# Where the eight turned pieces of a token block lie in PSUM, and how many last expert terms are summed at the end

## The chip, the cores and the metric

The kernel runs on one core of one Trainium2 chip. The metric is the device time of one execution in microseconds (us); the median of several executions is compared. Engines are named as in the profile: PE (TensorE, matmuls), PEld (its weight loads), DVE (VectorE), ACT (ScalarE), POOL (GpSimd) and SP (SyncE, which issues the DMAs). PSUM, the memory that PE writes, has eight banks of 512 f32 columns in each of 128 partitions.

## The reference, cut to what matters

256 tokens of width 1024 go through a first block (attention and mLSTM, then PEER, a sum over 128 x 128 experts) and through two layers of a second block (a mixer and a convolutional GLU, here "ffn"). Between any two of these stages stands the same join: the stage's output is added to the running tokens x, and x is normalised for the next stage.

```
def rmsnorm(x, g):
    y = xf * lax.rsqrt(jnp.mean(xf * xf, axis=-1, keepdims=True) + EPS)
    return (y * g.astype(jnp.float32)).astype(x.dtype)
...
        act = jax.nn.gelu(jnp.einsum('thkd,td->thk', expert_u[eidx], xb).astype(jnp.float32), approximate=False)
        return jnp.einsum('thk,thkd->td', (g * act).astype(xb.dtype), expert_v[eidx])
...
        x = x + gt2 * peer(h2, w_pq[l], sub_keys[l], expert_u[l], expert_v[l])
```

## The kernel before

Matmuls run in split precision: a number is held as a high and a low half, and `mm3` (L274 to L276) issues high x high, high x low and low x high as three matmuls; `mm` (L279) is a single one. The split of a weight is made by ACT (`wh`, L289) and DVE or POOL (`wl`, L293). `bank()` hands out one of the eight PSUM banks.

The join (L714 on) works on two blocks b of 128 tokens each. For each block `update` adds the stage's output to x (L741 to L749, DVE); `norm` squares x on ACT (`jj`, L724), makes 1/rms by a chain of ten small DVE operations (L731, then L402 to L410) and puts it on a diagonal matrix `jdg` on ACT (L759); `features` then multiplies each of eight 128 x 128 pieces of x by `jdg`, which turns the piece (features onto partitions) and scales it. Each piece goes to a bank of its own, ACT reads it there into the high half (L768: `hh`, in the join ahead of PEER `r`), and DVE reads it again for the low half (L778: `hl`; ahead of PEER, where a bias is added, the pair L782 and L783). There are five such joins with features: ahead of PEER (tiles `x`, in the profile at 264 to 283 us), ahead of the mixer of layer 0 and 1 (at 1107 and 1497 us), and ahead of the ffn of layer 0 and 1 (at 1300 and 1687 us); a sixth writes the output and turns nothing.

In the joins of the mixers and the ffns a first sum that needs the features (the mixer's values, with weights `sh`, `sl`; the ffn's first products, with `sth`, `stl`) is issued block by block within the join, as `early`: for the mixer 32 matmuls with `hh` and then 16 with `hl` in each block, for the ffn 16 and 8. The join ahead of PEER has none, and 15 plain matmuls of the identity (`warm`) stand there instead.

PEER ends with a sum over 128 terms into four banks (two token blocks by two halves of the columns). Its last `TAILV` terms are not summed as they come: their weights are split into four tiles each (`wtail`: two halves of `wth` and two of `wtl`, from a pool of 40 such tiles that 16 tiles of the next mixer's values share), and `finish` then sums bank after bank, so that the first token block is complete while the second is still summed. The activations of a term (`k`) lie in tiles of which there are six.

The order of the instructions on each engine is set by a list scheduler ahead of time; the `issue_after` lines at the end of `join` pin a few of them. A tile's buffer, a bank too, is taken again when its last user is done, and engines that use one bank are kept apart by semaphores.

Of the kernel before, what the change touches and what calls it, by code (L numbers as in the profile page):

```python
# [19 lines left out]
P = 128  # L20
# [24 lines left out]
WARM2 = 12  # L45
DLAG = 4
TAILF = 5
TAILV = 5
NRAW = 6
NWIDE = 40  # L50
AVF = 4, 6, 8, 10
# [208 lines left out]
class Kern:  # L260
# [453 lines left out]
    def join(self, ys, row, post, out=None, scale=None, bias=None, pair=None, early=None):  # L714
# [47 lines left out]
        def features(b):  # L762

            xs, o, low = self.X[2 * b:2 * b + 2], slice(b * P, (b + 1) * P), []
            for c in range(KD):
                pt = self.bank()[:, :P]
                self.mm(pt, xs[c // 4][:, c % 4 * P:(c % 4 + 1) * P], dgs[b])
                self.mark = nc.scalar.activation(hT[c].hi[:, o], pt, AF.Copy if bias is None else AF.Identity,  # L768
                                                 bias=0.0 if bias is None else bias[:, c:c + 1],
                                                 scale=scale[:, c:c + 1])  # L770
                low.append(pt)
            yield
            for c, pt in enumerate(low):
                if c == LOS:
                    yield
                hi, lo = hT[c].hi[:, o], hT[c].lo[:, o]
                if bias is None:
                    nc.vector.scalar_tensor_tensor(lo, pt, scale[:, c:c + 1], hi.bitcast(F32),  # L778
                                                   op0=OP.mult, op1=OP.subtract)
                else:  # L780
                    h32 = self.S([P, P], name="h32")
                    nc.vector.tensor_scalar(h32, pt, scale[:, c:c + 1], bias[:, c:c + 1], op0=OP.mult, op1=OP.add)  # L782
                    nc.vector.tensor_tensor(lo, h32, hi.bitcast(F32), op=OP.subtract)  # L783
            yield

        after = self.tc.issue_after
        dgs = []
        u0, u1, n0, n1, f0, f1 = update(0), update(1), norm(0), norm(1), features(0), features(1)
        next(u0)
        next(u0)  # L790
# [36 lines left out]
    def peer(self, ys, gb):  # L827
# [166 lines left out]
        for n, j in enumerate(order):  # L994
# [8 lines left out]
            hh = parted[n]  # L1003
            if n >= NKEY - TAILV:
                parts.append((hh, self.wtail(src)))
# [1029 lines left out]
```

## Time and profile before

| what | us |
|---|---|
| median of 3 executions (lowest, highest) | 1892.14 (1888.83, 1896.81) |
| the profiled execution | 1893.5 |
| its span in the trace | 1891.7 |
| PE busy in it | 1823.5 |
| DVE, ACT busy | 1305.4, 1004.2 |
| PE idle for `jdg` (L759), five times, in all | 15.0 |
| PE idle for `hl` (L778), four times, in all | 5.5 |

PE is the engine that is nearly always busy. What it idles is small, and a part of that idling lies in the five joins. In a timeline row the first number is the start, the second the length, then engine, line and operation, and at the end in brackets how long the engine had been idle and what released it.

### The profile page before, as it was taken

What the parts mean: (1) busy time and instruction counts of PE and PEld (TensorE: products, weight loads), DVE (VectorE), ACT (ScalarE), POOL (GpSimd) and SP (SyncE); (2) the same over time, 40 slices, a digit from 0 to 9 for tenths busy, and PEclk for the clock granted to TensorE, in tenths of its full rate; (3) what the DMA queues carried; (4) which work ended last, traced back from release to release, by engine and by line L of the source; (5) the groups of instructions that cost most, each with busy time, mean ns of one, the idle gap of its engine ahead of it and who ended that gap; (6) DMA issues with size and microseconds to landing.
All of it is one profiled execution on the core that took longest, in us unless ns stands there. A gap on an engine that the chain in (4) does not pass through costs nothing.

```text
span 1891.7 us, 32791 instructions
## 1 busy us (share of the span) xinstructions
PE 1823.5 (96%) x12634; PEld 1621.5 (86%) x12634; DVE 1305.4 (69%) x3029; ACT 1004.2 (53%) x1856; POOL 176.6 (9%) x119
## 2 busy tenths in 40 slices
PE   7999989999999999999999999998999999989998
PEld 6776579999999999888888788987999899879997
DVE  4535677997888896555555656767787666767775
ACT  4525544435666665444444646456666464456663
POOL 0000002321000000000000003400100033201000
PEclk9999989999999999999999999999999999999999
DMA  8722454454445446555555744313676233125571
GB/s 308 255 102 101 152 173 135 162 173 138 162 159 165 161 164 203 189 188 187 186 188 183 231 137 135 112 56 112 202 233 217 74 130 128 56 82 184 195 232 57
DMA packets 85101, 302.93 MB, mean 160 GB/s; under 512 B 10096, under 2 KB 10992, under 8 KB 84816
## 3 DMA queue, kind: packets, MB, share of 16 engines
q1 hardware_dynamic: 84944, 300.83, 48.1%
q8 instruction: 99, 1.62, 0.3%
q14 instruction: 58, 0.48, 0.1%
HBM read 298.56 MB, written 2.10 MB: 159 GB/s over the span
## 4 chain that ended last, share of the span: by engine, by line
PE 82%; DVE 12%; ACT 3%; DMA 1%; issue 1%; SPq 0%; POOLq 0%; POOL 0%; DVEq 0%; ACTq 0%
PE b L274 22%; PE b L276 21%; PE b L275 21%; PE b L279 14%; DVE wl L293 3%; PE b L1160 1%; DMA raw<-in_wv 1%; ACT wh L289 1%; PE b L524 1%; PE b L1351 1%; DMA raw<-in_w_ada 1%; DVE eq L1091 0%; DVE tm L1024 0%; DVE u L1980 0%; DVE jt L741 0%
## 5 line engine op out<-in xcount | busy, mean ns | idle before, releaser
L289 ACT ACTIVATE wh<-raw 128x1024 fp32r<-128x1024 f32 x457 | 483.7, 1060 | 532.0 <-PE b L275 214.4
L293 DVE TENSOR_TENSOR wl<-raw,wh 128x1024 fp32r<-128x1024 f32 x414 | 524.2, 1267 | 274.0 <-ACT wh L289 273.5
L276 PE MATMUL b<-r,wl 128*128 128x256 f32 (+1 forms) x1216 | 345.0, 284 | 9.1 <-DVE wl L293 9.1
L274 PE MATMUL b<-r,wh 128*128 128x256 f32 (+1 forms) x1216 | 351.9, 289 | 0.0
L275 PE MATMUL b<-r,wh 128*128 128x256 f32 x1152 | 323.7, 281 | 0.0
L274 PE MATMUL b<-hh,wh 128*128 128x256 f32 x1056 | 301.6, 286 | 1.8 <-DVE ast L1676 1.8
L276 PE MATMUL b<-hh,wl 128*128 128x256 f32 x1056 | 299.6, 284 | 1.8 <-DVE wl L293 1.7
L275 PE MATMUL b<-hl,wh 128*128 128x256 f32 x1056 | 298.6, 283 | 0.0
L276 PEld LDWEIGHTS b<-r,wl 128*128 128x128 f32 x1216 | 231.0, 190 | 11.8 <-DVE wl L293 10.3
L274 PEld LDWEIGHTS b<-r,wh 128*128 128x128 f32 x1216 | 231.1, 190 | 3.1 <-issue 1.5
L293 POOL TENSOR_TENSOR wl<-raw,wh 128x1024 fp32r<-128x1024 f32 x43 | 105.7, 2459 | 1219.5 <-ACT wh L289 947.8
L275 PEld LDWEIGHTS b<-r,wh 128*128 128x128 f32 x1152 | 218.6, 190 | 0.0
L274 PEld LDWEIGHTS b<-hh,wh 128*128 128x128 f32 x1056 | 202.2, 191 | 4.5 <-DVE ast L1676 2.2
L276 PEld LDWEIGHTS b<-hh,wl 128*128 128x128 f32 x1056 | 202.2, 191 | 3.1 <-DVE wl L293 3.0
L275 PEld LDWEIGHTS b<-hl,wh 128*128 128x128 f32 x1056 | 202.3, 192 | 1.4
L275 PE MATMUL b<-wl,k 128*128 128x512 f32 x492 | 194.9, 396 | 1.5 <-DVE wl L293 1.4
L274 PE MATMUL b<-wh,k 128*128 128x512 f32 x492 | 194.7, 396 | 0.0
L276 PE MATMUL b<-wh,k 128*128 128x512 f32 x492 | 194.6, 395 | 0.0
L275 PEld LDWEIGHTS b<-wl,k 128*128 128x128 f32 x492 | 92.4, 188 | 24.7 <-DVE wl L293 2.6
L274 PEld LDWEIGHTS b<-wh,k 128*128 128x128 f32 x492 | 92.4, 188 | 22.5 <-ACT wh L289 0.3
L276 PEld LDWEIGHTS b<-wh,k 128*128 128x128 f32 x492 | 92.4, 188 | 22.3
L1980 DVE SCALAR_TENSOR_TENSOR u<-b,vec,u 128x255 f32<-128x255 f32 (+1 forms) x176 | 84.3, 479 | 9.1 <-ACT u L1978 6.5
(492 smaller groups left out, 3019.0 us busy)
## 6 DMA issues: line engine op xcount, KB each, us to landing
raw<-in_eu SPq DMA_DIRECT2D x128, 512.0 KB, 3.8
raw<-in_ev SPq DMA_DIRECT2D x128, 512.0 KB, 3.6
raw<-in_fi SPq DMA_DIRECT2D x88, 512.0 KB, 4.6
raw<-in_w_ada SPq DMA_DIRECT2D x48, 512.0 KB, 5.3
raw<-in_wi SPq DMA_DIRECT2D x48, 512.0 KB, 3.9
raw<-in_fo SPq DMA_DIRECT2D x44, 512.0 KB, 4.7
raw<-in_w SPq DMA_DIRECT2D x16, 512.0 KB, 6.1
raw<-in_w_pq SPq DMA_DIRECT2D x16, 512.0 KB, 4.2
```

The lines of the kernel that those rows point to most:

```text
L274: mm(out, L.hi, R.hi, start=start, stop=False, skip_group_check=True)
L275: mm(out, L.hi, R.lo, start=False, stop=False, skip_group_check=True)
L276: self.lastmm = mm(out, L.lo, R.hi, start=False, stop=stop, skip_group_check=True)
L279: self.nc.tensor.matmul(out, l, r, start=start, stop=stop, skip_group_check=True)
L289: nc.scalar.activation(dst.hi, src, AF.Copy)
L293: e.tensor_tensor(dst.lo, src, dst.hi.bitcast(F32), op=OP.subtract)
L524: nc.tensor.matmul(pa[32 * j:32 * j + 32, :P], self.s2[:, 4 * h + k], wa[:, k, m * P:(m + 1) * P], start=(k == 0), stop=(k == 3), tile_pos ...
L1160: nc.tensor.matmul(pa[32 * j:32 * j + 32], self.s2[:, k], wa[:, j % 2 * 512:(j % 2 + 1) * 512], start=(k == 0), stop=(k == KD - 1), tile_p ...
L1351: nc.tensor.transpose(pt[:, sc * P:(sc + 1) * P], Pm[:, sc * P:(sc + 1) * P], self.ident)
L1980: nc.vector.scalar_tensor_tensor(u[:, g, j:], src[:, :T - j], self.v2("fc", (2 - j) * 44 + i), u[:, g, j:], op0=OP.mult, op1=OP.add)
```

## The change

The eight pieces of a token block no longer take eight banks: four of them lie side by side in one bank (`quad`), so that a block takes two. `TAILV` goes from 5 to 7: two more of PEER's terms are held back for `finish`. Line numbers behind the edit grow by two (L768 becomes L770, L778 L780, L782 and L783 L784 and L785).

```diff
-TAILV = 5
+TAILV = 7
...
             for c in range(KD):
-                pt = self.bank()[:, :P]
+                if c % 4 == 0:
+                    quad = self.bank()
+                pt = quad[:, c % 4 * P:(c % 4 + 1) * P]
                 self.mm(pt, xs[c // 4][:, c % 4 * P:(c % 4 + 1) * P], dgs[b])
```

The first place is PE's queue at the first token block of the join ahead of layer 0's mixer (`jdg` turns pieces; `sh` and `sl` by `hh` are the values; the number behind `b_` tells the bank's tile). Before:

```order
L279 MATMUL b_12161<-jdg_12157,r_9330 128x128 [waits Activation_49]
L279 MATMUL b_12164<-jdg_12157,r_9330 128x128
L279 MATMUL b_12167<-jdg_12157,r_9330 128x128 [waits PE_49]
L279 MATMUL b_12170<-jdg_12157,r_9330 128x128 [waits PE_49]
L279 MATMUL b_12173<-jdg_12157,r_9331 128x128 [waits DVE_49]
L279 MATMUL b_12176<-jdg_12157,r_9331 128x128
L279 MATMUL b_12179<-jdg_12157,r_9331 128x128 [waits DVE_49]
L279 MATMUL b_12182<-jdg_12157,r_9331 128x128 [waits DVE_49]
L279 MATMUL b_12214<-sh_11743,hh_12110 128x260 [waits DVE_49]
```

and now:

```order
L279 MATMUL b_12157<-jdg_12153,r_9318 128x128 [waits Activation_49]
L279 MATMUL b_12166<-jdg_12153,r_9319 128x128 [waits DVE_49]
L279 MATMUL b_12157<-jdg_12153,r_9318 128x128 [waits Activation_49]
L279 MATMUL b_12204<-sh_11731,hh_12106 128x260 [waits PE_49]
L279 MATMUL b_12204<-sl_11732,hh_12106 128x260
L279 MATMUL b_12205<-sh_11731,hh_12106 128x260 [waits PE_49]
L279 MATMUL b_12205<-sl_11732,hh_12106 128x260
L279 MATMUL b_12157<-jdg_12153,r_9318 128x128 [waits Activation_49]
L279 MATMUL b_12204<-sh_11735,hh_12108 128x260
L279 MATMUL b_12204<-sl_11736,hh_12108 128x260
```

The eight turning matmuls stood in a row, and each into its own bank; now the second piece of bank b_12157 waits for ACT, as do the third and all that follow in a bank, and matmuls of the values stand between them. Only the first piece of each of the two banks goes ahead without such a wait. The ffn's joins read likewise, with two matmuls (`sth`, `stl`) between pieces.

The second place is ACT's queue in the join ahead of PEER (L768, now L770, reads pieces; `wh` splits a weight; `jj` and `jdg` belong to the second token block). Before, from the sixth piece of the first block on:

```order
L724 ACTIVATE jj_2518,jss_2517<-x_77 128x512
L724 ACTIVATE jj_2520,jss_2517<-x_77 128x512 [waits DVE_49]
L289 ACTIVATE wh_2711<-raw_2709 128x1024 [waits DMAHW3_49]
L289 ACTIVATE wh_2744<-raw_2742 128x1024 [waits DMAHW4_49]
L289 ACTIVATE wh_2791<-raw_2789 128x1024 [waits DMAHW5_49]
L759 ACTIVATE jdg_2562<-ident_59,rq_2525 128x128 [waits DVE_49]
```

and now, from the third piece of the first block on:

```order
L770 ACTIVATE r_2436<-b_2477,mod1_1601,a2_2423 128x128 [waits PE_49]
L289 ACTIVATE wh_2779<-raw_2777 128x1024 [waits DMAHW5_49]
L770 ACTIVATE r_2437<-b_2477,mod1_1601,a2_2423 128x128 [waits PE_49]
L770 ACTIVATE r_2438<-b_2486,mod1_1601,a2_2423 128x128 [waits Activation_49]
L770 ACTIVATE r_2439<-b_2486,mod1_1601,a2_2423 128x128 [waits PE_49]
L770 ACTIVATE r_2440<-b_2486,mod1_1601,a2_2423 128x128 [waits PE_49]
L770 ACTIVATE r_2441<-b_2486,mod1_1601,a2_2423 128x128 [waits DVE_49,PE_49]
L724 ACTIVATE jj_2512,jss_2511<-x_77 128x512
L724 ACTIVATE jj_2514,jss_2511<-x_77 128x512 [waits DVE_49]
L759 ACTIVATE jdg_2556<-ident_59,rq_2519 128x128 [waits DVE_49]
```

The three splits `wh` stood behind the second block's squares; they now stand between the pieces of the first block. Their low halves on DVE stood among the ten small operations of the second block's norm; they now stand ahead of the first block's low halves, and the ten operations have only the last low halves among them. In the second block of this join the pieces of the two banks alternate (b_2558, b_2567, b_2558, and so on).

The third place is PE's queue in `finish`, where the seventh term comes in (`wth`, `wtl` are halves of its weights, `k1` its activations):

```order
L276 MATMUL b_9317<-wth_11925,k1_11918 128x512
L274 MATMUL b_9317<-wth_11938,k1_11931 128x512
L275 MATMUL b_9317<-wtl_11939,k1_11931 128x512
L276 MATMUL b_9317<-wth_11938,k1_11931 128x512
L274 MATMUL b_9314<-wth_11999,k1_11996 128x512 [waits Activation_49]
L275 MATMUL b_9314<-wtl_12000,k1_11996 128x512 [waits DVE_49]
L276 MATMUL b_9314<-wth_11999,k1_11996 128x512 [waits DVE_49]
L274 MATMUL b_9315<-wth_12003,k1_11996 128x512
L275 MATMUL b_9315<-wtl_12004,k1_11996 128x512
L276 MATMUL b_9315<-wth_12003,k1_11996 128x512
```

With five terms `finish` had 60 matmuls, bank by bank, without such a break. With seven it has 84: the seventh term's activations need the tile that the first of the rows shown reads last (six tiles for seven terms), so the term comes only after six terms of three banks and two terms of the fourth. 18 matmuls then follow the first token block's last one, instead of 30.

## Rows read from the trace of the kernel before

**Rows 1.** The page: busy time, share of the span and instructions of each engine.

```profile
PE 1823.5 (96%) x12634; PEld 1621.5 (86%) x12634; DVE 1305.4 (69%) x3029; ACT 1004.2 (53%) x1856; POOL 176.6 (9%) x119
```

**Rows 2.** PE's waits: waiter, releaser, us in all, times, longest.

```profile
PE b L279 <- ACT jdg L759: 15.0, 5, 7.3
...
PE b L279 <- DVE hl L778: 5.5, 4, 1.9
```

**Rows 3.** Timeline of PE, join ahead of layer 0's mixer (columns above).

```profile
1107.41 0.40 PE L276 MATMUL b<-wth,k 128*128 128x512 f32 x1
1110.68 2.05 PE L279 MATMUL b<-jdg,r 128*128 128x128 f32 x16 [2.88 <-ACT jdg L759]
...
1116.84 2.09 PE L279 MATMUL b<-sh,hl 128*128 128x260 f32 x16
1118.76 1.95 PE L279 MATMUL b<-jdg,r 128*128 128x128 f32 x16
...
1126.29 0.28 PE L274 MATMUL b<-hh,wh 128*128 128x256 f32 x1
```

**Rows 4.** Timeline of ACT, same join.

```profile
1107.19 0.63 ACT L724 ACTIVATE jj<-r 128x512 bf16<-128x512 f32 x1 [12.12 <-PE b L276]
...
1110.23 0.40 ACT L759 ACTIVATE jdg<-ident,rq 128x128 f32<-128x128 f32 x1 [1.70 <-DVE rq L410]
1111.21 2.18 ACT L768 ACTIVATE hh<-b,vec 128x128 fp32r<-128x128 f32 x8 [0.58 <-PE b L279]
1113.23 0.68 ACT L724 ACTIVATE jj<-r 128x512 bf16<-128x512 f32 x1
...
1116.23 0.40 ACT L759 ACTIVATE jdg<-ident,rq 128x128 f32<-128x128 f32 x1 [1.63 <-DVE rq L410]
...
1119.19 0.37 ACT L768 ACTIVATE hh<-b,vec 128x128 fp32r<-128x128 f32 x1 [0.80 <-PE b L279]
```

**Rows 5.** Timeline of DVE, same join.

```profile
1116.12 1.12 DVE L778 SCALAR_TENSOR_TENSOR hl<-b,vec,hh 128x128 fp32r<-128x128 f32 x4
```

**Rows 6.** Timelines of PE, then ACT, join ahead of layer 0's ffn.

```profile
1300.24 2.05 PE L279 MATMUL b<-jdg,r 128*128 128x128 f32 x16 [1.89 <-ACT jdg L759]
1304.19 0.39 PE L279 MATMUL b<-sth,hh 128*128 128x256 f32 x1 [1.89 <-DVE hl L778]
...
1311.94 0.38 PE L373 MATMUL b<-ident,tok 128*128 128x128 f32 x2
...
1300.77 2.18 ACT L768 ACTIVATE hh<-b,vec 128x128 fp32r<-128x128 f32 x8 [0.58 <-PE b L279]
...
1306.41 0.40 ACT L759 ACTIVATE jdg<-ident,rq 128x128 f32<-128x128 f32 x1 [1.78 <-DVE rq L410]
```

**Rows 7.** Timeline of PE, join ahead of layer 1's ffn: first turn and what follows the join.

```profile
1687.40 2.05 PE L279 MATMUL b<-jdg,r 128*128 128x128 f32 x16 [1.87 <-ACT jdg L759]
...
1700.45 0.38 PE L373 MATMUL b<-ident,tok 128*128 128x128 f32 x2
```

**Rows 8.** Stretches: length, busy PE, PEld, DVE, ACT, POOL (x), PEclk, DMA share, GB/s.

```profile
277.50:281.00 3.50, 3.46 (x17) 3.47 (x17) 2.27 (x9) 2.63 (x7) 0.00 (x0) 0.50 0.96 336
...
1692.50:1696.50 4.00, 4.00 (x23) 4.00 (x22) 2.31 (x13) 1.03 (x3) 0.00 (x0) 0.57 0.02 4
```

**Rows 9.** Timelines of PE, ACT and DVE, join ahead of PEER.

```profile
277.54 3.79 PE L279 MATMUL b<-jdg,x 128*128 128x128 f32 x16 [7.28 <-ACT jdg L759]
280.97 0.56 PE L274 MATMUL b<-r,wh 128*128 128x256 f32 x1
...
265.06 2.91 ACT L768 ACTIVATE r<-b,mod,a 128x128 fp32r<-128x128 f32 x8 [0.44 <-PE b L279]
...
277.08 0.40 ACT L759 ACTIVATE jdg<-ident,rq 128x128 f32<-128x128 f32 x1 [5.06 <-DVE rq L410]
278.37 3.44 ACT L768 ACTIVATE r<-b,mod,a 128x128 fp32r<-128x128 f32 x8 [0.89 <-PE b L279]
...
282.74 0.48 DVE L783 TENSOR_TENSOR r<-h,r 128x128 fp32r<-128x128 f32 x2
```

## The prediction

> **What bounds the kernel now.** I read the page first, then PE's waits, then the timelines of PE, ACT and DVE at the five joins and at the end of the experts' sum. PE is busy 96% of the span [rows 1], so a change of buffers can gain or lose only where PE idles. The edit touches two such places, the turning of the pieces in the joins and the end of PEER's sum. PE idles 15.0 us in five gaps for the diagonal `jdg`, and 5.5 us in four for a low half `hl` [rows 2]; the second is the reading of a bank that has to end before the next sum gets a bank, and is what more free banks can give back.
>
> In the mixer's join, eight pieces (two passes each, hence x16) take PE 2.05 us, and ACT reads them almost as fast, 2.18 us for eight, 0.27 each, from 0.53 us behind PE's start [rows 3, 4]. That works because PE writes one bank while ACT reads another. ACT then squares the second block at once (1113.23), whose `jdg` starts 3.00 us later, at 1116.23 [rows 4]. It comes 2.1 us too early: PE is in the first block's values until 1118.76 [rows 3]. So today the second norm is hidden, and that slack is what the change eats first.
>
> **One trip.** The order of the changed kernel shows each piece but a bank's first waiting for ACT to have read the one before. What a trip costs is in the rows: from a turning matmul's start to ACT's reading 0.43 us (1118.76 to 1119.19), the reading 0.37 to 0.38, from ACT's end back to PE 0.05 (1110.23 + 0.40 to 1110.68) [rows 3, 4]: **0.86 us**. At half clock the first part is 0.83 (277.54 to 278.37) [rows 9], which makes about 1.3. Eight pieces on ACT were 8 x 0.27 = 2.18; now the first block's are three trips, a step of 0.27 to the second bank (whose first piece is ready), and three trips: the last reading starts 6 x 0.86 + 0.27 = 5.43 us behind the first and ends at 5.81, so **3.63 us later** than 2.18. Values matmuls stand between, but only two to four of 0.12 us each (2.09 us for 16 [rows 3] less the overlap), which fit into a trip and don't lengthen it.
>
> Here the Trainium skill bears on the case: the page "PSUM — Partial Sum Buffer", section "PSUM bank collisions raise a hardware error", says that accesses of two engines to one bank have to be ordered whatever columns they touch, and "Perfetto Trace Analysis", section "Matmuls", wants independent matmuls to rotate through banks so that one's evacuation overlaps the next. The trace agrees with the second (2.05 beside 2.18 us on eight banks). The same PSUM page of the Trainium skill, in "The four PSUM rules", lets four 128 x 128 transposes be packed in one bank, which concerns the accumulation flags; no run here shows what that costs in time, and were the packing free, the rival of the freed banks would hold.
>
> **Mixers' joins (two).** First reading at 1111.21 as before, last one ends at 1117.0. ACT's squares for the second block follow it as before, so `jdg` goes from 1116.23 to 1119.9 and ends at 1120.3; the 2.1 us of slack are used up and 1.5 us are over (1120.3 against 1118.76). PE meanwhile has high-half products left, then waits: the low halves of the second bank stand behind the ten norm operations on DVE, and four of them take 1.12 [rows 5], so they end near 1121.1. In the second block the order has a bank's pieces mostly one behind the other, again about six trips with the first reading at 1120.7: last reading starts at 1125.9. 15 `hh` and 16 `hl` matmuls still stand behind that on PE, 31 x 0.12 = 3.7, so the join ends near 1129.8 against 1126.29 [rows 3]: **+3.5 each, +7.0**. If the second block hid its trips wholly it would be +1.5; if nothing overlapped, 3.63 + 3.63 less the 2.1 of slack, +5.
>
> **ffn's joins (two).** Last reading of the first block again 3.63 later, at 1306.6 for 1302.95. The squares waited 0.3 us for x there, so `jdg` moves from 1306.41 to about 1309.7, +3.3 [rows 6]. The gap of 1.89 us ahead of the first product (1304.19) goes away, since a bank is free; but what it gives is spent inside the trips, because PE cannot pass the turning matmuls. In the second block the two banks' pieces alternate: four trips of two, first reading 1310.6, last 3 x 0.86 + 0.27 later and ended by 1313.9, four low halves of 1.12 in all until 1315.1, the last `hl` products behind them until about 1315.6, against 1311.94 [rows 6]: **+3.7 each, +7.4**. Between +1.8 (the 1.89 kept in full) and +5.5 (it was needed anyway).
>
> **PEER's join.** ACT now has three splits `wh` between the first pieces (about 1.0 us each, so a bank's first four readings take 4 us), then four readings with three trips at a clock that is falling. That puts the last reading of the first block at 273 to 274 for 267.8 (265.06 + 2.91 less the overlap), and the squares and the ten operations, free of `wl` splits now, give `jdg` at 276.5 to 278, against 277.08 [rows 9]. Before, that chain waited among the splits, 5.06 us on ACT and 7.28 on PE [rows 9]. The second block is four trips of two at the 0.50 clock that the stretch had [rows 8]: 1.3 x 3 + 0.8 + 0.27 + 0.46 = 5.5 to the last reading's end where it was 4.7 (277.08 to 281.81). Its low halves come after their bank is full, in pairs of 0.72 + 0.48, so PE's products begin near 283 instead of 280.97, and their 48 matmuls are paced by them. **+2**, between -1 and +4: the lower end if `jdg` comes early and the clock is whole, the upper if it comes at 278 and the clock stays at half.
>
> **TAILV 7.** Two terms fewer of `wh`/`wl` in the common stream, four halves each more in the tail; ACT and DVE do as much. The seventh term's activations wait for a tile that PE frees three matmuls (0.23 us each) ahead; a split on ACT and DVE takes about 0.9 us, so PE may wait some tenths. The first block is complete 18 matmuls (4.2 us) ahead of the end for 30 (7.0), and its update on DVE still fits. The squares waited until 1107.19 for a tile that PE releases 3 matmuls from the end (12.12 us idle [rows 4]); the order still has that distance, so the 2.88 us until `jdg` [rows 3] stay. **+0.2**, from -0.3 to +1.
>
> **Clock.** The two ffn joins are alike in order, but layer 1's takes 13.05 us (1687.40 to 1700.45) and layer 0's 11.70 [rows 6, 7], the former with a granted clock of 0.57 for 4 us [rows 8], behind gaps of 1.87 and 1.89 us. So a fall costs **1.35 us** in such a join. The change makes four joins thinner for PE; I take one more fall, +1.35, and 0 to 4 of them, 5.4, for the bounds.
>
> **Sum.** 7.0 + 7.4 + 2 + 0.2 + 1.35 = **+18 us**. The profiled execution took 1893.5 us, 1.4 above the median of 1892.14, which I take as scatter: 1911.5 for it, **1910** for a median. What follows each join is PE-bound products, so nothing behind it takes the delay up.
>
> **Rivals.** *Overlap hides half*: the mixers' second blocks hide their trips (+1.5 each), the ffns keep their 1.89 (+1.8 each), PEER +1, one fall or none: 3 + 3.6 + 1 = +8, **1900**. For it: 0.12 us products stand between trips; against: the order puts them where the low halves, not the trips, are late. *Freed banks win* (the faster side): if a piece need not wait for the reading before it, the trips vanish, the two gaps of 1.89 go (3.8), and PEER's 7.28 falls to about the 2.88 of a mixer (4.4): -8.2, **1884**. It decides from a trip below about 0.4 us; the rows' 0.86 and the waits in the order speak against it. *The clock falls in all joins*: four times 1.35, and seven trips of 1.3 for 0.86 in one or two of the blocks, PEER at +4: about +30, **1922**. For it: the fall is seen in one of two equal joins already; against: products now fill what were gaps. *The longer tail does nothing or stalls*: within +-1, in the range.
>
> **How the numbers follow.** Forecast 0.62 (1903 to 1917 for itself), half hidden 0.19, freed banks 0.06, clock 0.13. The range leaves out freed banks, some of the half hidden and the upper end of the clock: 1897 to 1924. About 0.5%, 9.5 us, is what a measurement of this kernel can tell from no change, so slower begins at 1901.6: it holds all of clock, nearly all of the forecast and a part of the half hidden case (0.77); faster is part of freed banks (0.04); the rest, 0.19, is between.
>
> **What would show it.** ACT's eight readings should be no longer one group of 2.18 us but eight 0.86 us apart, each released by PE, and PE's turning matmuls by ACT; the second `jdg` 3.3 to 3.7 us later behind the first in mixers and ffns; the 1.89 us gap of the ffns gone; joins of 19.1 (mixer, from 1110.68) and 15.4 us (ffn, from 1300.24) instead of 15.6 and 11.7; PEER's wait for `jdg` about as long, its products 2 us later; the sum's end without a gap over 0.5 us. A trip well under 0.8 us, or products that begin before the pieces are through, would make it wrong on the low side; a granted clock near 0.5 in the mixers' joins on the high side.

## The result and the profile after

The changed kernel takes 1917.6 us in the median of six executions (1911.78 to 1921.81) against 1889.17 for the kernel before: a ratio of 1.0138 (95% interval 1.012 to 1.0155), which is 26 us; the two medians themselves lie 28.4 us apart. The profiled execution took 1921.81 us, with a span of 1920.0 against 1891.7, 28.3 more. One thing about the times has to be known: executions of one and the same kernel lie up to 14 us apart (1885.66 to 1899.34 for the kernel before), and in single profiles most of that stands in PEER's experts (810 to 820 us, last section); so lengths of joins are compared below, and not spans alone.

The stretches of the joins, of before and then of after, give the whole of it. Each row is one stretch: start and end, its length, the busy time of PE, PEld, DVE, ACT and POOL with their instructions, the granted PE clock, the DMA share and GB/s. The five rows are PEER's join (first turn to the first product with the keys), the mixer's and the ffn's join of layer 0, and those of layer 1 (first turn to the next stage's products; in the ffns' joins to the third of these, since the first two stand among the last products of the join). The sixth row, put second, is all of PEER's experts.

```profile
264.64:287.56 22.92, 15.59 (x111) 15.20 (x110) 17.26 (x50) 11.19 (x25) 2.45 (x1) 0.78 0.52 164
287.56:1107.41 819.85, 809.02 (x5544) 733.89 (x5542) 601.87 (x1384) 432.32 (x770) 45.61 (x18) 0.99 0.54 178
1110.68:1126.29 15.61, 15.44 (x128) 15.25 (x129) 7.79 (x31) 7.98 (x25) 2.39 (x1) 1.00 0.01 5
1300.24:1312.77 12.53, 10.61 (x86) 10.15 (x87) 10.99 (x42) 8.86 (x25) 0.00 (x0) 1.00 0.00 1
1496.89:1513.90 17.01, 15.45 (x129) 15.26 (x129) 8.88 (x40) 8.10 (x25) 2.39 (x1) 1.00 0.02 4
1687.40:1701.28 13.88, 11.97 (x87) 11.58 (x87) 11.00 (x42) 8.89 (x25) 0.00 (x0) 0.88 0.01 1
```

```profile
264.68:292.96 28.28, 18.63 (x111) 16.63 (x110) 17.49 (x50) 11.90 (x25) 2.88 (x1) 0.70 0.41 133
292.96:1112.15 819.19, 808.15 (x5544) 732.62 (x5542) 601.84 (x1386) 432.72 (x772) 45.32 (x18) 1.00 0.55 178
1115.42:1137.22 21.80, 20.64 (x129) 18.78 (x129) 7.88 (x31) 9.06 (x25) 2.42 (x1) 0.85 0.00 1
1311.20:1331.42 20.22, 17.70 (x86) 15.14 (x87) 10.48 (x42) 9.84 (x25) 0.00 (x0) 0.66 0.00 1
1515.55:1535.49 19.94, 18.56 (x128) 16.09 (x129) 9.07 (x40) 9.07 (x25) 2.39 (x1) 1.00 0.00 1
1709.04:1729.69 20.65, 18.36 (x87) 15.69 (x87) 10.54 (x42) 9.92 (x25) 0.00 (x0) 0.67 0.00 1
```

The joins grew by 5.4 (PEER), 6.2 and 2.9 (mixers), 7.7 and 6.8 us (ffns), 28.9 in all; the experts, with the longer tail, are 0.7 shorter. That is the 28.3. PE is "busy" through most of the growth, since the rows of its matmuls get longer in the trips (one turn by itself 0.49 us at the higher clock and 0.80 at the lower, where eight in a row took 2.05), and a long row counts as busy: its idle time grew by only 4.6 us (span less busy time, 72.8 for 68.2). These two waits of PE show no growth either, and would mislead anyone who looked only at them (against [rows 2]):

```profile
PE b L279 <- ACT jdg L759: 14.3, 5, 6.7
...
PE b L279 <- DVE hl L780: 5.3, 4, 1.6
```

The trips show on ACT. This is its timeline in the join ahead of layer 1's mixer, the one at full clock, where [rows 4] had one row of eight readings in 2.18 us:

```profile
1516.07 0.37 ACT L770 ACTIVATE hh<-b,vec 128x128 fp32r<-128x128 f32 x1 [0.58 <-PE b L279]
1517.02 0.37 ACT L770 ACTIVATE hh<-b,vec 128x128 fp32r<-128x128 f32 x1 [0.58 <-PE b L279]
...
1518.91 0.63 ACT L770 ACTIVATE hh<-b,vec 128x128 fp32r<-128x128 f32 x2 [0.58 <-PE b L279]
1520.12 0.37 ACT L770 ACTIVATE hh<-b,vec 128x128 fp32r<-128x128 f32 x1 [0.58 <-PE b L279]
...
1522.01 0.37 ACT L770 ACTIVATE hh<-b,vec 128x128 fp32r<-128x128 f32 x1 [0.58 <-PE b L279]
...
1525.23 0.40 ACT L759 ACTIVATE jdg<-ident,rq 128x128 f32<-128x128 f32 x1 [1.63 <-DVE rq L410]
```

Three trips, a double reading where the second bank's first piece was ready, three trips: the shape foretold, with 0.945 us a trip (the trips between the rows shown are at 1517.96 and 1521.06). In the ffn's join of layer 0 the clock falls while the trips run, and one takes 1.25; then PE waits for a low half (timelines of ACT, then of PE):

```profile
1313.91 0.37 ACT L770 ACTIVATE hh<-b,vec 128x128 fp32r<-128x128 f32 x1 [0.86 <-PE b L279]
1315.16 0.63 ACT L770 ACTIVATE hh<-b,vec 128x128 fp32r<-128x128 f32 x2 [0.89 <-PE b L279]
...
1322.85 0.58 PE L279 MATMUL b<-sth,hl 128*128 128x256 f32 x1 [1.43 <-DVE hl L780]
```

The gap of 1.89 us for a bank [rows 6] is gone, and this one of 1.43 stands in its stead: the second bank's low halves are behind the norm's ten operations, which are behind the last reading.

In PEER's join (timelines of ACT, DVE, POOL, DVE again and PE) the last reading of the first block starts at 273.11, the second `jdg` at 279.28, and the second block's first low half on DVE at 285.10:

```profile
273.11 0.46 ACT L770 ACTIVATE r<-b,mod,a 128x128 fp32r<-128x128 f32 x1 [0.89 <-PE b L279]
...
279.28 0.40 ACT L759 ACTIVATE jdg<-ident,rq 128x128 f32<-128x128 f32 x1 [4.50 <-DVE rq L410]
...
268.95 4.51 DVE L293 TENSOR_TENSOR wl<-raw,wh 128x1024 fp32r<-128x1024 f32 x2
...
269.49 2.88 POOL L293 TENSOR_TENSOR wl<-raw,wh 128x1024 fp32r<-128x1024 f32 x1 [269.05 <-ACT wh L289]
...
277.10 0.20 DVE L731 TENSOR_SCALAR jtt<-jss 128x1 f32<-128x1 f32 x1
...
285.10 0.73 DVE L784 TENSOR_SCALAR h<-b,a,mod 128x128 f32<-128x128 f32 x2 [5.85 <-ACT r L770]
...
286.08 0.58 PE L275 MATMUL b<-r,wh 128*128 128x256 f32 x1 [0.87 <-DVE r L785]
```

### The profile page after: what moved, and what is told of

Its sections match the earlier page's. It is cut to its first block, busy times and chain, and to the rows that moved or that the text cites. A ratio compares the mean times of both kernels' runs of the same rounds, so it can differ in the third digit from the quotient of the medians.

```text
span 1920.0 us, 32794 instructions
## 1 busy us (share of the span) xinstructions
PE 1847.2 (96%) x12634; PEld 1634.9 (85%) x12634; DVE 1305.4 (68%) x3031; ACT 1009.2 (53%) x1858; POOL 176.6 (9%) x119
## 4 chain that ended last, share of the span: by engine, by line
PE 82%; DVE 11%; ACT 3%; DMA 2%; issue 1%; SPq 0%; POOLq 0%; POOL 0%; DVEq 0%; ACTq 0%
PE b L274 21%; PE b L276 21%; PE b L275 21%; PE b L279 15%; DVE wl L293 3%; PE b L1162 1%; DMA raw<-in_wv 1%; PE b L524 1%; PE b L1353 1%; ACT wh L289 1%; ACT jj L724 1%; DVE eq L1093 0%; DVE tm L1026 0%; DVE u L1982 0%; PE b L1879 0%
## 5 line engine op out<-in xcount | busy, mean ns | idle before, releaser
L276 PEld LDWEIGHTS b<-r,wl 128*128 128x128 f32 x1216 | 231.0, 190 | 12.1 <-DVE wl L293 10.5
L274 PE MATMUL b<-wh,k 128*128 128x512 f32 x484 | 191.7, 396 | 0.0
L276 PE MATMUL b<-wh,k 128*128 128x512 f32 x484 | 191.4, 396 | 0.0
```

What stands on the lines that cost most here:

```text
L274: mm(out, L.hi, R.hi, start=start, stop=False, skip_group_check=True)
L276: self.lastmm = mm(out, L.lo, R.hi, start=False, stop=stop, skip_group_check=True)
```

## The experiments

The theory was that the whole loss is in the joins, and in the trips there; its rivals, that the longer tail takes part, that sharing a bank costs by itself, that the clock is the cause and the trips a by-product, that free banks are what counts. All ratios are to the kernel before, with 95% intervals. The list scheduler orders each version anew, so every run changes the order of some instructions along with what its edit says.

**The two halves of the change apart.** `t7_only` keeps a bank for each piece and takes only the tail:

```diff
-TAILV = 5
+TAILV = 7
```

> Seven held-back terms, every turned piece still in a bank of its own. Trips theory (all of the loss is in the joins): the joins as before, the experts' sum about 0.7 us shorter as in the changed kernel's trace (the end of the sum moved by 4.74 us there against 5.40 behind PEER's join), so 0 to -1.5 us against before, about 1888.5. Tail theory (the longer tail costs part of the 28): +3 us or more.

1.0004 (0.9987 to 1.0022): no difference. Its joins ahead of PEER and the mixers are those of before to 0.2 us; the ffns' are 0.8 and 0.3 us longer in its profile, at a granted clock of 0.87 and 0.76 where the profile of before has 1.00 and 0.88. So the clock in a join can differ from one profile to the next without any change to the join. `quad_t5` is the changed kernel with

```diff
-TAILV = 7
+TAILV = 5
```

> Four pieces to a bank, five held-back terms. Trips theory: the whole loss stays, 27 to 30 us over before, 1916 to 1919. Tail theory: clearly less than the change, 1910 or below.

1.0147 (1.0115 to 1.018), 1920.52 us: the whole loss, and a little more than foretold. The tail is out of the case. The wait at the seventh term shows in the changed kernel's timeline of PE as a single step of 0.31 us in `finish` (1106.74 to 1107.05), where 0.23 is the rule. In the profile of `quad_t5` the four joins of mixers and ffns together lose 23.7 us, as in the change (23.6), though layer 1's mixer now runs at 0.92 and the ffns at 0.74.

**The trips taken away, the shared banks kept.** `four_ahead` writes a bank's four matmuls ahead of its four readings:

```diff
                 if c % 4 == 0:
                     quad = self.bank()
-                pt = quad[:, c % 4 * P:(c % 4 + 1) * P]
-                self.mm(pt, xs[c // 4][:, c % 4 * P:(c % 4 + 1) * P], dgs[b])
+                    for i in range(4):
+                        self.mm(quad[:, i * P:(i + 1) * P], xs[c // 4][:, i * P:(i + 1) * P], dgs[b])
+                pt = quad[:, c % 4 * P:(c % 4 + 1) * P]
```

> Four pieces to a bank and seven terms as changed, but the four matmuls of a bank are written ahead of its four readings, so that no matmul waits for a reading of the piece before. Trips theory: the joins fall back to about the lengths of before (15.6 us mixers, 11.7 ffns), and the ffns lose their 1.9 us gap for a bank: 1884 to 1892. Rival (a shared bank costs by itself, because ACT and DVE cannot read it at once or because reading waits for the fourth piece): still 10 us or more over before, 1900 or above.

0.9982 (0.9963 to 1.0001), 1886.3 us: the loss is gone, with the same banks, the same instructions in another order and the same tail. Its stretches of PEER's join, then of the joins of layers 0 and 1:

```profile
263.01:283.94 20.93, 16.99 (x112) 16.50 (x110) 15.47 (x50) 10.69 (x25) 5.12 (x1) 0.76 0.56 180
...
1097.03:1113.64 16.61, 16.61 (x128) 16.61 (x129) 7.79 (x31) 8.01 (x25) 2.43 (x1) 0.91 0.00 1
1287.66:1302.16 14.50, 12.20 (x87) 11.79 (x87) 10.37 (x42) 8.61 (x25) 0.00 (x0) 0.88 0.01 1
1486.29:1501.47 15.18, 15.18 (x129) 15.18 (x129) 8.88 (x40) 7.89 (x25) 2.40 (x1) 1.00 0.00 1
1675.47:1688.80 13.33, 12.14 (x87) 11.73 (x87) 10.39 (x42) 8.62 (x25) 0.00 (x0) 0.87 0.00 1
```

So in the mixers' and ffns' joins together sharing costs next to nothing (0.6 us); what costs is to write and read a shared bank by turns. The mixers' joins hold no idle time of PE. The ffns' did not come out as foretold: layer 0's takes 14.50 us for 12.53 before. The gap of 1.89 us for a bank is gone there, but PE waits 1.95 us (1295.64) for a low half instead, and the clock is 0.88. PEER's join is 2.0 us shorter than before, and not by the missing trips alone: its second `jdg` comes 4.4 us earlier behind the first turn (7.99 for 12.44), since no `wl` split stands among that norm's operations any more (two stand behind them).

**Fewer trips.** `alternate` gives even pieces to one bank and odd ones to the other, so that a trip in one runs beside a trip in the other:

```diff
-            for c in range(KD):
-                if c % 4 == 0:
-                    quad = self.bank()
-                pt = quad[:, c % 4 * P:(c % 4 + 1) * P]
+            quads = [self.bank() for _ in range(2)]
+            for c in range(KD):
+                pt = quads[c % 2][:, c // 2 * P:(c // 2 + 1) * P]
```

> The changed kernel, but a block's pieces go to its two banks by turns (even pieces one, odd ones the other), so that one bank is read while the other is written. The first block then has three trips in series instead of six: last reading ends 3 x 0.95 + 0.27 + 0.37 = 3.5 us behind the first instead of 6.3 (2.2 before). Trips theory: the loss falls with the trips, to about a third to a half of 28: 1898 to 1904. Rival (two banks for eight pieces cost by themselves, however they are filled): 1912 or above.

1.0024 (1.0006 to 1.0042), 1897.3 us, a little better than expected. `pairs` puts two pieces in a bank, one behind the other:

```diff
-                if c % 4 == 0:
+                if c % 2 == 0:
                     quad = self.bank()
-                pt = quad[:, c % 4 * P:(c % 4 + 1) * P]
+                pt = quad[:, c % 2 * P:(c % 2 + 1) * P]
```

> The changed kernel with two pieces to a bank, four banks for a block. ACT's queue takes both pieces of a bank one behind the other, so the first block has four trips with three ready first pieces between them: 4 x 0.95 + 3 x 0.27 + 0.37 = 5.0 us for the readings. Trips theory: between the alternating banks and the change, 1904 to 1911, though it uses twice the banks. Rival (number of free banks decides): better than the alternating one, below 1898.

1.0041 (1.0022 to 1.006), 1898.92 us, clearly better than expected. By the medians the two can't be told apart, as their intervals overlap; the joins of their profiles show the order that trips give and banks don't. In the four joins of mixers and ffns, where the first block has three trips in series with two banks, four with four banks and six in the change, the loss is 7.8, 10.5 and 23.6 us. In these stretches (`alternate`: both layers' mixer and ffn in turn; `pairs` the same) the clock is 0.89 to 1.00 rather than the change's 0.66 to 1.00, and so part of the step from four trips to six is clock:

```profile
1107.54:1125.37 17.83, 17.60 (x129) 17.09 (x129) 7.88 (x31) 9.21 (x25) 2.43 (x1) 0.90 0.00 1
1299.36:1314.85 15.49, 13.11 (x86) 11.85 (x87) 10.46 (x42) 9.86 (x25) 0.00 (x0) 0.89 0.00 1
1498.97:1516.99 18.02, 17.79 (x128) 17.02 (x129) 9.06 (x40) 8.90 (x25) 2.40 (x1) 0.91 0.00 1
1690.99:1706.49 15.50, 13.17 (x87) 12.06 (x87) 10.48 (x42) 9.81 (x25) 0.00 (x0) 0.89 0.01 1
```

```profile
1103.14:1121.90 18.76, 18.11 (x128) 17.14 (x129) 7.96 (x31) 8.60 (x25) 2.44 (x1) 0.91 0.01 3
1295.96:1312.46 16.50, 13.48 (x87) 12.08 (x87) 10.83 (x42) 9.60 (x25) 0.00 (x0) 0.90 0.00 1
1496.57:1514.30 17.73, 17.07 (x128) 15.72 (x129) 8.97 (x40) 8.61 (x25) 2.39 (x1) 1.00 0.01 3
1688.36:1704.88 16.52, 13.51 (x87) 12.10 (x87) 10.86 (x42) 9.64 (x25) 0.00 (x0) 0.90 0.00 1
```

Where `pairs` missed its forecast is PEER's join, which is as long as before (23.07 for 22.92); `alternate` loses 3.75 there. I had not worked that join out for either, and took the share of the change.

**The clock apart from the trips.** `quad_gap` is the changed kernel with plain matmuls in PE's gap ahead of the first turn of the four joins:

```diff
         next(n0)
+        if early is not None:
+            with after(self.mark.ins):
+                self.warm(8)
```

> The changed kernel with eight plain matmuls (2.05 us) of the identity in PE's gap ahead of the first turn in the four joins of mixers and ffns. Clock theory (the gap and the thin stretch behind it let the clock fall to half, and that makes 10 or more of the 28 us): granted clock near 1 in these joins, their lengths those of layer 1's mixer (+2.9 to +3.7 over before), about 10 us less than the change, 1905 to 1910. Trips alone, clock a by-product: no more than 3 us less, 1914 to 1919.

1.0113 (1.0079 to 1.0147), 1913.22 us, between the two forecasts; the median alone doesn't decide between them. The stretches (mixer and ffn of layer 0, then of layer 1):

```profile
1112.66:1132.63 19.97, 18.59 (x128) 16.11 (x129) 7.88 (x31) 9.07 (x25) 2.42 (x1) 1.00 0.00 1
1305.95:1323.27 17.32, 13.17 (x86) 10.85 (x87) 10.39 (x42) 9.81 (x25) 0.00 (x0) 1.00 0.00 1
1507.96:1527.81 19.85, 18.48 (x131) 16.01 (x130) 8.54 (x38) 9.07 (x25) 2.39 (x1) 1.00 0.00 1
1701.57:1720.78 19.21, 15.06 (x87) 13.25 (x87) 10.72 (x42) 9.94 (x25) 0.00 (x0) 0.82 0.00 1
```

Three of the four joins now run at full clock, and lose 4.4, 4.8 and 2.8 us to before, not 6.2, 7.7 and 2.9; the fourth, still at 0.82, loses 5.3 for 6.8. So of 23.6 us in these joins some 6 are the clock, and 17 the trips with what stands behind them. The 6 are more than scatter: the change, `quad_t5` and `quad_no_peer` below lose 23.6, 23.7 and 23.0 us in the same joins. Nor do the plain matmuls only move the time ahead of the first turn: from the last product to it the four joins take 3.27, 2.01, 2.01 and 2.04 us, for 3.27, 2.25, 1.47 and 2.26. The clock is a part, but it comes on top: with the clock whole, most of the loss stays.

**PEER's join apart.** `quad_no_peer` shares banks only where there is no bias:

```diff
-                if c % 4 == 0:
+                if bias is not None or c % 4 == 0:
                     quad = self.bank()
-                pt = quad[:, c % 4 * P:(c % 4 + 1) * P]
+                pt = quad[:, :P] if bias is not None else quad[:, c % 4 * P:(c % 4 + 1) * P]
```

> The changed kernel, but the join ahead of PEER keeps a bank for each piece. If the joins add up, PEER's 5.4 us go and the rest stays: 1911 to 1914, and PEER's join as long as before (22.9 us from its first turn to the first product with the keys, against 28.3). If PEER's loss were made elsewhere (the order of splits is set by something other than the banks), 1916 or above.

1.013 (1.0096 to 1.0163), 1916.29 us. The median is over the 1911 to 1914 of the additive case, and just inside the other (1916 or above), and four executions that lie 6 us apart (1911.61 to 1918.0) can't tell 5 us. The profile can: PEER's join is as long as before, and the other four lose 23.0 us, as in the change (23.6).

```profile
266.71:289.42 22.71, 15.38 (x112) 15.00 (x111) 17.26 (x50) 11.19 (x25) 2.45 (x1) 0.85 0.52 166
```

So the joins add up by their profiles; by the medians this stays open.

**A version that beats both.** `four_gap` is `four_ahead` with the same eight plain matmuls in the gap as `quad_gap`.

> Four matmuls of a bank ahead of its readings, and eight plain matmuls in the gap ahead of the first turn of the mixers' and ffns' joins. With no trips left, what remains over before in the profile of the version without plain matmuls is the clock (granted 0.88 to 0.91 in three of the four joins). Clock theory: 3 to 5 us below that version, 1881 to 1884, faster than before. Rival: the plain matmuls do nothing or are in the way: 1886 to 1890.

0.9959 (0.9938 to 0.998), 1884.08 us beside 1890.63: some 7 us faster than before, at the upper edge of the 1881 to 1884 of the clock theory. The joins of layer 0 and of layer 1:

```profile
1106.95:1122.13 15.18, 15.18 (x128) 15.18 (x129) 7.79 (x31) 7.90 (x25) 2.43 (x1) 1.00 0.00 1
1295.98:1310.49 14.51, 12.76 (x86) 11.94 (x87) 10.84 (x42) 8.72 (x25) 0.00 (x0) 0.88 0.01 1
1495.17:1510.24 15.07, 15.07 (x131) 15.07 (x129) 8.36 (x38) 7.89 (x25) 2.40 (x1) 1.00 0.00 1
1683.58:1696.60 13.02, 11.27 (x86) 10.46 (x87) 10.35 (x42) 8.51 (x25) 0.00 (x0) 1.00 0.00 1
```

By its ratio it is 0.23 per cent, 4.3 us, below `four_ahead`, as the clock theory has it, but the two intervals overlap. In the profiles less of it is seen: the mixer and the ffn whose clock came back from 0.91 and 0.87 gained 1.4 and 0.3 us, and the ffn of layer 0, still at 0.88, nothing; in layer 1's mixer the plain matmuls put the first turn off by 0.5 us. Against before, PEER's join gives 2.4 us and the mixers' 2.4, and the ffns' take 1.1; the other half of the 7 us isn't placed.

## Why the prediction came out as it did

The direction, the mechanism and the range held: 1917.6 lies in 1897 to 1924, and the loss is where it was put. But the forecast itself, +18, was too low, and the result, +26 (28.3 in the profile), is nearer to the rival in which the clock falls in all joins (+30). By terms (at full clock means as in `quad_gap`):

| term | forecast | profile | why |
|---|---|---|---|
| mixers' joins | +7.0 | +9.1 | 4.4 and 2.8 at full clock, the rest clock |
| ffns' joins | +7.4 | +14.5 | 4.8 at full clock in layer 0, 5.3 at 0.82 in layer 1; the rest clock |
| PEER's join | +2 | +5.4 | see below |
| seven terms | +0.2 | -0.7, within the scatter of the experts; alone 0 (`t7_only`) | right: 0.08 us of waiting |
| clock, extra | +1.35 | within the above, about 6 in four joins | mis-sized |

Of the 10.3 us between the forecast and the profile, what `quad_gap` gave back (6.3, of which 1.35 were foretold) makes 4.9, PEER's join 3.4, and what `quad_gap` left in the ffns' joins 2.7; the tail and the mixers make up the rest. The mixers' term came out near (7.2 as in `quad_gap`) by luck, since two misses nearly cancel: 4.4 in layer 0 for 3.5, with longer trips than put, and 2.8 in layer 1, where the kernel before had an idle stretch of 1.56 us ahead of its first values (1500.50), which the change took away and the prediction did not see.

**The trip** was put at 0.86 us and takes 0.945 at full clock. The way back from ACT to PE, taken from the wait for `jdg`, held (0.05). The way out, from the turn's start to the reading, was taken from a turn that follows other matmuls without a break (0.43); in a trip PE starts anew after a pause, and it takes 0.52, as the first turn of the join did (0.53 in [rows 3, 4]). Together they are the 0.58 that ACT idles in every trip. Six of them and the pair make 0.5 us more for a block. The prediction had three trips, a step to the second bank and three trips, and the rows show just that; the second `jdg` of layer 1's mixer is 3.85 us later behind the first turn (9.68 for 5.83), for 3.63.

**The step that failed is the clock.** I priced a fall by what it cost the kernel before in one ffn join (1.35 us [rows 7, 8]) and took one more. In the changed joins a fall costs more, since the trips themselves get longer (1.25 for 0.945), and it came in three of the four joins; before, one of these three had it. PEER's join has it in both (0.78 before, 0.70 now). I had the longer trip in the text and used it only for PEER and for the rival. "Products now fill what were gaps" was the reason against the rival; the windows show the opposite, 0.66 and 0.67 in the ffns. What makes the clock fall in one profile of a join and not in another stays open.

**PEER's join**: the last reading came where it was put (273 to 274), the second `jdg` did not (279.28 for 276.5 to 278). The ten operations of the norm lost the `wl` splits among them, but those now stand ahead of all of the first block's low halves, and those ahead of the norm: it starts at 277.10. Two splits took DVE 4.51 us there, while POOL was in a split of its own for 2.88 (269.49); one by itself takes 1.22. Before, a small operation on DVE that takes 0.16 elsewhere had been stretched in the same way (timelines of DVE and POOL before the change):

```profile
271.13 1.22 DVE L293 TENSOR_TENSOR wl<-raw,wh 128x1024 fp32r<-128x1024 f32 x1
272.26 2.31 DVE L407 SCALAR_TENSOR_TENSOR rq<-rq 128x1 f32<-128x1 f32 x1
...
272.10 2.45 POOL L293 TENSOR_TENSOR wl<-raw,wh 128x1024 fp32r<-128x1024 f32 x1 [271.66 <-DMA x_wait<-x]
```

That the two get in each other's way is read from such rows only, and no run sets them apart; in `four_ahead` it was POOL's split that grew, to 5.12 us (271.14), beside two on DVE in their usual 2.35 (271.09). Two products began at 281.5 and 282.9, and the unbroken row of them at 286.08, for "near 283". The term's upper end, +4, was passed.

The late `jdg` is not the whole of it, though, and the join is long without it too. Of the 5.4 us, 2.2 lie ahead of the second `jdg` and 3.2 behind it. The second block's first low half on DVE comes 5.8 us behind the second `jdg`, when the seventh of the eight readings is done; before it came 1.8 us behind, as soon as a first piece had been read. In `alternate` the second `jdg` is 1.0 us earlier behind the first turn than before (11.41 for 12.44), the low half again 5.8 us behind it, and the join is 3.75 us longer. In `quad_t5`, where the splits on DVE were not stretched, the `jdg` is only 0.6 us late, and the join still takes 28.1 us; the products behind it ran at a granted clock of 0.63, for 0.78 in the change. In `pairs`, where a bank is full after two pieces, the low half comes 3.1 us behind `jdg`, and the join is as long as before. The first row is from before the change, the other two from `alternate`:

```profile
278.86 0.84 DVE L782 TENSOR_SCALAR h<-b,a,mod 128x128 f32<-128x128 f32 x2 [1.22 <-ACT r L768]
```

```profile
276.49 0.40 ACT L759 ACTIVATE jdg<-ident,rq 128x128 f32<-128x128 f32 x1 [4.01 <-DVE rq L410]
...
282.30 0.41 DVE L783 TENSOR_SCALAR h<-b,a,mod 128x128 f32<-128x128 f32 x1 [4.53 <-ACT r L769]
```

So in PEER's join the second reader, DVE, which in these rows gets at a shared bank only when all its pieces have been written and read, is a cost of sharing beside the trips. The prediction had this ("low halves come after their bank is full") and put the products some 6 us behind `jdg`; they came 6.8 behind it. No run changes this order alone, so its share of the 3.2 us is argued and not shown.

**The ffns' gap**: right that 1.89 us would be spent inside the trips; not foreseen that a new wait of 1.43 for the second bank's low halves would stand behind them.

**The rules of the Trainium skill**: "Perfetto Trace Analysis", section "Matmuls", of the Trainium skill wants independent matmuls to rotate through banks so that one's evacuation overlaps the next. The runs agree: two banks by turns (`alternate`) lose only a third of what two banks in sequence lose in the joins of mixers and ffns (7.8 of 23.6 us), and `four_ahead` shows that two banks are enough when they rotate by four matmuls at a time. The order of accesses to one bank that "PSUM — Partial Sum Buffer" of the Trainium skill asks for, in the section "PSUM bank collisions raise a hardware error", is what makes the trips: the change waits for it at every piece. `four_ahead` keeps it, with one wait for four pieces, and has none.

## What to carry to other kernels

Before tiles share a bank, look at the order in which they are written and read: write, read, write, read into one bank costs a round trip for each piece (0.95 us here, for a reading of 0.27), while all writes ahead of all reads cost next to nothing in these joins and free the banks. If a second engine reads the bank too, ask when it gets at it. Price a round trip at both clocks of TensorE, because three of the four joins with trips ran below the higher one, and multiply by the number in series. When a change has two halves, measure each alone: here the tail was worth nothing.

## What I had not expected of the hardware

TensorE's clock fell from its higher to its lower level (2.4 to 1.2 GHz) for part of two joins that had run at 1.00 before, layer 0's mixer and ffn (0.85 and 0.66 over the join), behind the same gaps of 2.9 and 1.9 us. Eight plain matmuls in that gap brought both back to 1.00, and layer 1's ffn from 0.67 to 0.82. And the experts' first stage, which no edit touches, ran at two paces, at a granted clock of 1.00 in both: 934 matmuls in 100 us in the profile of before, 962 in that of `pairs`. The change and `t7_only` ran at the first pace, `quad_gap` and `four_ahead` at the second. What sets that pace is open; it makes most of the 7.8 us between the profiles of before and `pairs` in the experts (819.9 and 812.0 us).

```profile
490.00:590.00 100.00, 100.00 (x934) 98.93 (x933) 85.22 (x205) 63.93 (x140) 0.00 (x0) 1.00 0.49 164
```

```profile
490.00:590.00 100.00, 100.00 (x962) 99.12 (x962) 87.47 (x213) 66.41 (x147) 0.00 (x0) 1.00 0.50 169
```
